# Attention values on Trainium2: float32 products on half of the array's columns for each head parity, in groups of four jobs

## The chip, the cores and the metric

The kernel runs on one core of one Trainium2 chip. A core has a matrix engine (TensorE: PE for its matmuls, PEld for its weight loads), three engines for elementwise work (VectorE: DVE; ScalarE: ACT; GpSimd: POOL) and an engine that issues transfers (SyncE: SP). Each engine works through its own queue in order and waits on semaphores for the others. The metric is the time of one execution on the device in microseconds (us); lower is better.

## The reference, cut to what matters

One decoder layer for 1024 tokens: a normalised input is projected, half of the heads go through sparse attention, the other half through a gated delta rule; an output projection and a gated MLP follow. The change concerns the attention. Each query sees three sets of keys: compressed blocks, selected blocks, and a window of 512 tokens. Each set has its own softmax, its own gate and its own values:

```
p_cmp = masked_softmax(einsum('bqhgd,bhnd->bhgqn', qb, kc), m_cmp)
o_cmp = einsum('bhgqn,bhnd->bqhgd', p_cmp, vc)
p_sel = masked_softmax(einsum('bqhgd,bhqnd->bhgqn', qb, k_sel), m_sel)
o_sel = einsum('bhgqn,bhqnd->bqhgd', p_sel, v_sel)
p_win = masked_softmax(einsum('bqhgd,bkhd->bhgqk', qb, kw), m_win)
o_win = einsum('bhgqk,bkhd->bqhgd', p_win, vw)
o = gate_cmp * o_cmp + gate_sel * o_sel + gate_win * o_win
```

There are 8 query heads of 64 numbers in 2 groups (g), each group with one key and one value head. All is float32.

## The kernel before, in words

The program goes through the stages input projections and delta rule, attention, output projection, MLP up, MLP down. In the attention a *unit* is 128 queries (tile i) of one group g with its four heads: 16 units, from tile 7 down to tile 0. `phase_attend` runs several units at once, one behind the other: `select` (compressed scores and the choice of blocks) of unit n+3, `scores` (the scores and softmax of the window and of the selection) of unit n+1, `values` of unit n, the norm of a finished tile, and `out_gdn` or `out_nsa` (part of the output projection, tile `og_ps`) as filler. `interleave` mixes them, and a scheduler then orders each engine's queue from what every instruction needs and from priorities; listings of that order stand with the change.

`values` gets the gated softmax rows as [128 queries, keys] and needs them with the keys on the partitions. Its work is a list of *jobs*: job 0 is the 64 compressed keys, then one job for each 128 keys of the window, then one for each 128 keys of the selection; 3 jobs for tile 0 up to 14 for tile 7, 148 in all units. A job before the change: four transposes on PE (L880, one a head) into one PSUM bank `pt` (three banks in rotation); ACT copies it rounded to the fast matmul format (L882, `ph`); DVE subtracts that copy from the bank to keep the rest (L890, `pl`; L885 for job 0); then PE does two products of 512 columns (L891 with `ph`, L892 with `pl`; L886 for job 0) into the one accumulator bank `po`. The values `vst` hold 128 columns: 64 rounded and 64 of the rest, so the two products give all four part products. At the end of a unit the halves of `po` are added and put into `oT` by head parity (heads 0 and 2 on partitions 0 to 63, heads 1 and 3 on 64 to 127): ACT copies one half or both (L897, L904), DVE or POOL adds (L899, L906).

The values are prepared before the attention: `v_raw` is loaded in four transfers, ACT rounds it (L613), POOL subtracts (L614). For the compressed values `compress` does the same from PSUM with ACT and DVE (L717, L718).

The delta rule uses plain float32 products too: `kk_ps` (L285) multiplies on one half of the array's columns for each half c of a token tile, and `u_ps` (L384) on all columns. A plain float32 product is two records of PE in the trace, each with a weight load of its own.

Of the kernel before, what the change touches and what calls it, by code (L numbers as in the profile page):

```python
# [9 lines left out]
F32 = mybir.dt.float32  # L10
F32R = mybir.dt.float32r
BF16 = mybir.dt.bfloat16
AF = mybir.ActivationFunctionType
ALU = mybir.AluOpType
# [4 lines left out]
P = 128  # L19
SEQ = 1024  # L20
NT = SEQ // P
# [487 lines left out]
def phase_in(K, ctx):  # L509
# [91 lines left out]
    K.vst = vp.tile([P, NT, 2, 2, P], F32R, name="vst")  # L601
# [6 lines left out]
    vr = scr.enter_context(tc.tile_pool(name="vraw", bufs=4, side="right"))  # L608
    for j in range(4):
        raw = vr.tile([P, 2, 2, 2, 64], F32, name="v_raw", tag="v_raw")  # L610
        nc.sync.dma_start(raw.rearrange("p t b g d -> p t (b g d)"), K.d_v[:, 2 * j:2 * j + 2, :])
        d = slice(2 * j, 2 * j + 2)
        nc.scalar.activation(K.vst[:, d, :, :, 0:64], raw, AF.Copy)  # L613
        nc.gpsimd.tensor_tensor(out=K.vst[:, d, :, :, 64:128], in0=raw, in1=K.vst[:, d, :, :, 0:64].bitcast(F32),  # L614
                                op=ALU.subtract)
# [46 lines left out]
def compress(K, which, pool):  # L662
# [47 lines left out]
    else:  # L710
        for h in range(2):
            vp = K.pp.tile([64, 64], F32, name="vc_ps", tag="proj")
            for j in range(2):
                nc.tensor.matmul(vp, x[:, j, 64 * h:64 * h + 64], w2[:, j, :], start=(j == 0), stop=(j == 1))

            for d in (slice(0, 64), slice(64, 128)):
                nc.scalar.activation(K.vc[d, h, 0:64], vp, AF.Copy, scale=0.5)  # L717
                nc.vector.scalar_tensor_tensor(out=K.vc[d, h, 64:128], in0=vp, scalar=0.5,  # L718
                                               in1=K.vc[0:64, h, 0:64].bitcast(F32), op0=ALU.mult, op1=ALU.subtract)
# [147 lines left out]
def values(K, i, g, U):  # L867

    nc = K.nc
    pc, pw, pn, lo = U.pc, U.pw, U.pn, U.lo  # L870
    po = K.p_o.tile([P, 4, P], F32, name="po", tag="po")
# [5 lines left out]
    for n, (src, v, kk) in enumerate(jobs):  # L877
        pt = K.p_t.tile([P, 4, P], F32, name="pt", tag="pt")
        for h in range(4):
            nc.tensor.transpose(pt[0:kk, h, :], src[h], K.ident)  # L880
        ph = K.apl.tile([P, 4, P], F32R, name="ph", tag="ph", bufs=3)
        nc.scalar.activation(ph[0:kk], pt[0:kk], AF.Copy)  # L882
        if n == 0:

            nc.vector.tensor_tensor(out=ph[kk:P], in0=pt[0:kk], in1=ph[0:kk].bitcast(F32), op=ALU.subtract)  # L885
            nc.tensor.matmul(po, v, ph, start=True, stop=False)  # L886
            yield
            continue
        pl = K.apl.tile([P, 4, P], F32R, name="pl", tag="pl", bufs=3)
        nc.vector.tensor_tensor(out=pl, in0=pt, in1=ph.bitcast(F32), op=ALU.subtract)  # L890
        nc.tensor.matmul(po, v, ph, start=False, stop=False)  # L891
        nc.tensor.matmul(po, v, pl, start=False, stop=(n == len(jobs) - 1))  # L892
        yield

    if i < 4:
        lo_ = K.apl.tile([64, 4, P], F32, name="po_s", tag="po_s", bufs=1)
        nc.scalar.activation(lo_, po[64:128], AF.Copy)  # L897
        for par in range(2):
            nc.vector.tensor_tensor(out=U.oT[64 * par:64 * par + 64, 2 * g:2 * g + 2, :], in0=po[0:64, par::2, :],  # L899
                                    in1=lo_[:, par::2, :], op=ALU.add)  # L900
        return
    hh = K.apl.tile([64, 2, 4, P], F32, name="po_s", tag="po_s", bufs=1)
    for j in range(2):
        nc.scalar.activation(hh[:, j], po[64 * j:64 * j + 64], AF.Copy)  # L904
    for par in range(2):
# [641 lines left out]
```

## Time and profile before

| | |
|---|---|
| time, median of 3 runs | 1500.3 us (1497.18 to 1500.89) |
| the profiled execution's own time | 1502.3 us |
| its span in the profile | 1500.5 us |
| PE busy | 1420.9 us (95%) |
| DVE busy | 1153.7 us (77%) |
| ACT busy | 723.3 us (48%) |
| POOL busy | 575.3 us (38%) |
| mean granted TensorE clock | 0.977 of full |

The span is the time from the first to the last instruction of the profiled execution; its own time is 1.8 us longer. Busy PE time includes the time in which a matmul drains while the next streams, so 95% doesn't mean that no time is left. The attention's values stand between 503 us (first transpose of `values`) and 792 us (last addition into `oT`) of the span.

### The profile page before, as it was taken

What the parts mean: (1) busy time and instruction counts of PE and PEld (TensorE: products, weight loads), DVE (VectorE), ACT (ScalarE), POOL (GpSimd) and SP (SyncE); (2) the same over time, 40 slices, a digit from 0 to 9 for tenths busy, and PEclk for the clock granted to TensorE, in tenths of its full rate; (3) what the DMA queues carried; (4) which work ended last, traced back from release to release, by engine and by line L of the source; (5) the groups of instructions that cost most, each with busy time, mean ns of one, the idle gap of its engine ahead of it and who ended that gap; (6) DMA issues with size and microseconds to landing.
All of it is one profiled execution on the core that took longest, in us unless ns stands there. A gap on an engine that the chain in (4) does not pass through costs nothing.

```text
span 1500.5 us, 21074 instructions
## 1 busy us (share of the span) xinstructions
PE 1420.9 (95%) x7260; PEld 1163.8 (78%) x7260; DVE 1153.7 (77%) x2222; ACT 723.3 (48%) x1405; POOL 575.3 (38%) x567
## 2 busy tenths in 40 slices
PE   8998899999989999989998979999999999989997
PEld 8876677787877777777787858888888888778886
DVE  5768997886335788898975797888888888687656
ACT  7443343232233566788865544444444445333333
POOL 3355433344352245466563541111111112364444
PEclk9999999999999999999999989999999999999999
DMA  6245352444366543132215112323222235773333
GB/s 234 87 156 177 107 169 72 125 121 150 93 219 173 161 138 112 58 85 52 55 64 200 40 70 105 105 105 106 105 94 98 97 105 194 268 267 87 103 106 147
DMA packets 106059, 188.04 MB, mean 125 GB/s; under 512 B 17216, under 2 KB 52064, under 8 KB 105952
## 3 DMA queue, kind: packets, MB, share of 16 engines
q1 hardware_dynamic: 105952, 186.69, 38.5%
q8 instruction: 57, 0.93, 0.3%
q14 instruction: 50, 0.41, 0.1%
HBM read 135.00 MB, written 51.66 MB: 124 GB/s over the span
## 4 chain that ended last, share of the span: by engine, by line
PE 64%; DVE 19%; DMA 6%; ACT 4%; issue 4%; POOL 2%; SPq 1%; DVEq 0%; ACTq 0%; POOLq 0%
PE up_ps L1130 27%; PE dn_ps L1328 11%; PE proj_ps L128 3%; PE proj_ps L126 3%; PE proj_ps L127 3%; DVE cv_acc L465 3%; PE pt L880 2%; DVE pl L890 2%; PE po L892 1%; DVE zb L350 1%; PE po L891 1%; DVE ztmp L348 1%; PE s_ps L820 1%; PE s_ps L415 1%; DMA d_x<-og 1%
## 5 line engine op out<-in xcount | busy, mean ns | idle before, releaser
L1328 PE MATMUL dn_ps<-d_op 128*128 128x512 f32 x924 | 211.4, 390 | 5.7 <-DVE d_op L1322 3.8
L1328 PEld LDWEIGHTS dn_ps<-d_op 128*128 128x128 f32 x924 | 173.0, 188 | 43.6 <-DVE d_op L1322 5.0
L128 PE MATMUL proj_ps<-hH,w_l 128*128 128x512 f32 x384 | 158.3, 412 | 6.6 <-POOL w_l L118 6.6
L126 PE MATMUL proj_ps<-hH,w_h 128*128 128x512 f32 x384 | 156.2, 408 | 5.0 <-ACT cv_acc L463 3.2
L127 PE MATMUL proj_ps<-hL,w_h 128*128 128x512 f32 x384 | 155.3, 405 | 0.1
L1320 POOL TENSOR_TENSOR d_op<-a_raw,d_op 128x1024 fp32r<-128x1024 f32 (+1 forms) x42 | 104.7, 2496 | 123.0 <-ACT d_op L1319 105.6
L1130 PE MATMUL up_ps<-th,op_h 128*128 128x512 f32 x336 | 133.5, 398 | 7.1 <-ACT op_h L1154 7.1
L1130 PE MATMUL up_ps<-th,op_l 128*128 128x512 f32 x336 | 133.6, 398 | 3.6 <-DVE op_l L1156 3.6
L1130 PE MATMUL up_ps<-tl,op_h 128*128 128x512 f32 x336 | 133.3, 397 | 0.0
L118 POOL TENSOR_TENSOR w_l<-w_raw,w_h 128x1024 fp32r<-128x1024 f32 (+2 forms) x46 | 110.1, 2398 | 46.1 <-ACT w_h L116 44.5
L1322 DVE TENSOR_TENSOR d_op<-b,d_op 128x1024 fp32r<-128x1024 f32 (+1 forms) x42 | 80.8, 1928 | 48.5 <-ACT d_op L1321 42.1
L1130 PE MATMUL up_ps<-dl,op_h 128*128 128x512 f32 x288 | 113.8, 395 | 0.0
L1130 PE MATMUL up_ps<-dh,op_h 128*128 128x512 f32 x288 | 112.6, 395 | 1.0 <-ACT acc L167 1.0
L1130 PE MATMUL up_ps<-dh,op_l 128*128 128x512 f32 x288 | 110.5, 394 | 0.0
L882 ACT ACTIVATE ph<-pt 128x512 fp32r<-128x512 f32 (+1 forms) x148 | 85.3, 591 | 49.1 <-PE pt L880 41.3
L1242 DVE SCALAR_TENSOR_TENSOR ga<-f_g,vec,ga 128x1024 f32<-128x1024 f32 x44 | 89.3, 2029 | 16.9 <-ACT ga L1240 16.3
L890 DVE TENSOR_TENSOR pl<-pt,ph 128x512 fp32r<-128x512 f32 x132 | 89.5, 683 | 9.1 <-ACT ph L882 8.6
L128 PEld LDWEIGHTS proj_ps<-hH,w_l 128*128 128x128 f32 x384 | 74.6, 194 | 26.9 <-POOL w_l L118 10.6
L1154 ACT ACTIVATE op_h<-w_raw 128x1024 fp32r<-128x1024 f32 (+1 forms) x64 | 59.0, 923 | 74.8 <-PE up_ps L1130 69.7
L1319 ACT ACTIVATE d_op<-a_raw 128x1024 fp32r<-128x1024 f32 (+1 forms) x42 | 41.4, 988 | 108.7 <-PE dn_ps L1328 53.8
L1175 POOL MEMSET f_u<- 128x2 f32 x22 | 2.2, 100 | 234.0 <-DVE acc L1242 233.1
L126 PEld LDWEIGHTS proj_ps<-hH,w_h 128*128 128x128 f32 x384 | 74.6, 195 | 21.2 <-ACT cv_acc L463 4.9
(343 smaller groups left out, 3654.6 us busy)
## 6 DMA issues: line engine op xcount, KB each, us to landing
w_raw<-in_w_up_dram SPq DMA_DIRECT2D x44, 512.0 KB, 3.2
a_raw<-d_a SPq DMA_DIRECT2D x35, 512.0 KB, 3.6
w_raw<-in_w_gdn_dram SPq DMA_DIRECT2D x24, 512.0 KB, 3.5
d_a<-ga SPq DMA_DIRECT2D x44, 256.0 KB, 2.0
b<-in_w_down_dram SPq DMA_DIRECT2D x20, 512.0 KB, 6.9
d_a<-so SPq DMA_DIRECT2D x33, 256.0 KB, 2.0
qT<-d_q SPq DMA_DIRECT2D x32, 256.0 KB, 4.8
mg<-d_mix SPq DMA_DIRECT2D x16, 512.0 KB, 3.7
```

Of the source, the lines that this page charges most:

```text
L118: (low or nc.gpsimd).tensor_tensor(out=wl, in0=raw, in1=wh.bitcast(F32), op=ALU.subtract)
L126: nc.tensor.matmul(out, ah, bh, start=(i == 0), stop=False)
L127: nc.tensor.matmul(out, ah, bl, start=False, stop=False)
L128: nc.tensor.matmul(out, al, bh, start=False, stop=(i == n - 1))
L882: nc.scalar.activation(ph[0:kk], pt[0:kk], AF.Copy)
L890: nc.vector.tensor_tensor(out=pl, in0=pt, in1=ph.bitcast(F32), op=ALU.subtract)
L1130: mm = lambda a, b, start, stop: nc.tensor.matmul(out, a, b, start=start, stop=stop, skip_group_check=not first)
L1154: nc.scalar.activation(h, src, AF.Copy)
L1242: nc.vector.scalar_tensor_tensor(out=a, in0=raw[:, j:j + SEQ], scalar=tap(j), in1=a, op0=ALU.mult, op1=ALU.add)
L1320: nc.gpsimd.tensor_tensor(out=al, in0=raw, in1=ah.bitcast(F32), op=ALU.subtract)
L1322: nc.vector.tensor_tensor(out=bl, in0=b[js.start], in1=bh.bitcast(F32), op=ALU.subtract)
L1328: one = lambda a, b, start, stop: nc.tensor.matmul(ps, a, b, start=start, stop=stop, skip_group_check=not first)
```

## The change

The value products become plain float32. `vst` holds the values once, 64 columns wide, and is filled by one transfer; `vc` holds the compressed values as 64 by 64 and is written by ACT alone. In `values` a transposed bank `pt` is copied once as float32 (`pT`), by DVE for the first job of each four and by ACT for the others. A product is split by head parity: heads 0 and 2 go with the value columns to partitions 0 to 63 of `po`, heads 1 and 3 to 64 to 127, each 256 columns wide. So `po` is already laid out as `oT`, and one copy by ACT ends the unit. The products of four jobs are issued one behind the other, newest job first, held in that order and with raised priority.

```
-    K.vst = vp.tile([P, NT, 2, 2, P], F32R, name="vst")
+    K.vst = vp.tile([P, NT, 2, 2, 64], F32, name="vst")
+    nc.sync.dma_start(K.vst.rearrange("p t b g d -> p t (b g d)"), K.d_v)
...
-    for j in range(4):
-        raw = vr.tile([P, 2, 2, 2, 64], F32, name="v_raw", tag="v_raw")
-        nc.sync.dma_start(raw.rearrange("p t b g d -> p t (b g d)"), K.d_v[:, 2 * j:2 * j + 2, :])
-        d = slice(2 * j, 2 * j + 2)
-        nc.scalar.activation(K.vst[:, d, :, :, 0:64], raw, AF.Copy)
-        nc.gpsimd.tensor_tensor(out=K.vst[:, d, :, :, 64:128], in0=raw, in1=K.vst[:, d, :, :, 0:64].bitcast(F32),
-                                op=ALU.subtract)
...
-            for d in (slice(0, 64), slice(64, 128)):
-                nc.scalar.activation(K.vc[d, h, 0:64], vp, AF.Copy, scale=0.5)
-                nc.vector.scalar_tensor_tensor(out=K.vc[d, h, 64:128], in0=vp, scalar=0.5,
-                                               in1=K.vc[0:64, h, 0:64].bitcast(F32), op0=ALU.mult, op1=ALU.subtract)
+            nc.scalar.activation(K.vc[:, h], vp, AF.Copy, scale=0.5)
...
-    po = K.p_o.tile([P, 4, P], F32, name="po", tag="po")
+    po = K.p_o.tile([P, 2, P], F32, name="po", tag="po")
...
-        ph = K.apl.tile([P, 4, P], F32R, name="ph", tag="ph", bufs=3)
-        nc.scalar.activation(ph[0:kk], pt[0:kk], AF.Copy)
...
-        pl = K.apl.tile([P, 4, P], F32R, name="pl", tag="pl", bufs=3)
-        nc.vector.tensor_tensor(out=pl, in0=pt, in1=ph.bitcast(F32), op=ALU.subtract)
-        nc.tensor.matmul(po, v, ph, start=False, stop=False)
-        nc.tensor.matmul(po, v, pl, start=False, stop=(n == len(jobs) - 1))
...
+    last, left = None, len(jobs)
+    for n0 in range(0, len(jobs), 4):
+
+        todo = []
+        for n in range(n0, min(n0 + 4, len(jobs))):
+            src, v, kk = jobs[n]
+            pt = K.p_t.tile([P, 4, P], F32, name="pt", tag="pt")
+            for h in range(4):
+                nc.tensor.transpose(pt[0:kk, h, :], src[h], K.ident)
+            pT = K.apl.tile([P, 4, P], F32, name="pT", tag="pT", bufs=2 * 4)
+            if n % 4 in (0,):
+                nc.vector.tensor_copy(pT[0:kk], pt[0:kk])
+            else:
+                nc.scalar.activation(pT[0:kk], pt[0:kk], AF.Copy)
+            todo.insert(0, (v, pT[0:kk]))
             yield
...
+        with tc.high_priority(offset=100):
+            for v, pT in todo:
+                left -= 1
+                for par in range(2):
+                    with tc.issue_after(last.ins) if last else nullcontext():
+                        last = nc.tensor.matmul(po[64 * par:64 * par + 64], v, pT[:, par::2], start=(last is None or first),
+                                                stop=(left == 0))
+                    first = par == 0 and left == len(jobs) - 1
+    nc.scalar.activation(U.oT[:, 2 * g:2 * g + 2, :], po, AF.Copy)
```

**PE in the first unit.** Before the change PE's queue stands so where the first jobs of tile 7's first unit are worked off (`pt` transposes, `po` value products, `s_ps` scores of the next unit, `og_ps` filler):

```order
L880 MATMUL pt<-ident,p_win 128x128 x4
L820 MATMUL s_ps<-kst_4414,qT 128x256
L822 MATMUL s_ps<-kst_4414,qT 128x256
L880 MATMUL pt<-ident,p_win 128x128 x4
L886 MATMUL po<-ph,vc 128x512
L891 MATMUL po<-ph,vst 128x512
L880 MATMUL pt<-ident,p_win 128x128 x4
L892 MATMUL po<-pl,vst 128x512
L891 MATMUL po<-ph,vst 128x512
L126 MATMUL og_ps<-w_h,mg 128x512
```

Now it stands so behind the transposes of the same unit's first four jobs (line numbers of the changed kernel: L877 transposes, L890 value products, one for each parity):

```order
L127 MATMUL og_ps<-w_l,mg 128x512
L128 MATMUL og_ps<-w_h,mg 128x512
L877 MATMUL pt<-ident,p_win 128x128 x4
L890 MATMUL po<-pT,vst 64x256 x6
L890 MATMUL po<-pT,vc 64x256 x2
L877 MATMUL pt<-ident,p_win 128x128 x4
L877 MATMUL pt<-ident,p_sel 128x128 x8
L809 MATMUL s_ps<-kst_4408,qT 128x384
L811 MATMUL s_ps<-kst_4408,qT 128x384
```

The two products of a job, which stood between transposes one job after its transposes, have become eight half-width products in one run, behind the transposes of the next group's first job. In the whole program PE has 41 such runs with 296 products; most hold four jobs.

**ACT at the end of a unit.** Before, where one unit ends and the next begins (`ph` copies of jobs, `po_s` the two halves of the accumulator, `p_win` softmax rows):

```order
L882 ACTIVATE ph<-pt 128x512
L904 ACTIVATE po_s<-po 64x512 x2
L838 ACTIVATE p_win,sums<-p_win,nmax 128x640
L882 ACTIVATE ph<-pt 128x512
L963 ACTIVATE mg<-mix 128x4x128
L882 ACTIVATE ph<-pt 128x512
L913 ACTIVATE sq<-oT 128x512
```

Now:

```order
L882 ACTIVATE pT<-pt 128x512
L741 ACTIVATE pc,sums<-pc,nmax 128x64 x2
L893 ACTIVATE oT<-po 128x256
L899 ACTIVATE sq<-oT 128x512
L882 ACTIVATE pT<-pt 128x512
L827 ACTIVATE p_win,sums<-p_win,nmax 128x640
```

The two copies of `po` are one of half the width that writes `oT` itself, and `sq`, the first step of the norm, stands right behind it; it no longer waits for an addition on another engine.

## Rows read from the trace of the kernel before

**Rows 1.** Windows: us, busy PE, PEld, DVE, ACT, POOL (x instructions), clock, DMA.

```profile
650.00:700.00 50.00, 46.30 (x292) 38.46 (x290) 46.10 (x154) 43.16 (x114) 32.19 (x44) 1.00 0.17 43
503.00:792.00 289.00, 267.78 (x1590) 222.55 (x1588) 247.94 (x810) 211.92 (x538) 149.44 (x217) 0.99 0.30 86
```

**Rows 2.** Groups by line, 503 to 792: busy us, mean ns, idle before.

```profile
L890 DVE TENSOR_TENSOR pl<-pt,ph 128x512 fp32r<-128x512 f32 x132 | 89.5, 683 | 9.1 <-ACT ph L882 8.6
L882 ACT ACTIVATE ph<-pt 128x512 fp32r<-128x512 f32 x132 | 76.8, 592 | 45.5 <-PE pt L880 38.0 <-PE po L886 6.1 <-DVE pl L890 0.5
...
L885 DVE TENSOR_TENSOR ph<-pt,ph 64x512 fp32r<-64x512 f32 x16 | 11.0, 685 | 1.4 <-ACT ph L882 1.0
...
L904 ACT ACTIVATE po_s<-po 64x512 f32<-64x512 f32 x16 | 9.5, 591 | 0.9 <-PE po L892 0.8
...
L899 DVE TENSOR_TENSOR oT<-po,po_s 64x256 f32<-64x256 f32 x16 | 6.6, 414 | 0.7 <-ACT po_s L897 0.6
...
L897 ACT ACTIVATE po_s<-po 64x512 f32<-64x512 f32 x8 | 4.8, 596 | 1.6 <-PE po L892 1.4
```

**Rows 3.** Waits of PE and PEld, 503 to 792: us in total, times, longest.

```profile
PE po L892 <- DVE pl L890: 6.8, 8, 1.9
PE pt L880 <- DVE og L952: 3.1, 4, 1.8
PE pt L880 <- DVE pl L890: 2.9, 3, 1.5
...
PEld po L892 <- DVE pl L890: 12.5, 18, 2.2
PEld pt L880 <- DVE pl L890: 2.6, 2, 1.7
```

**Rows 4.** Timeline around one stall: start us, us, engine, line.

```profile
663.30 0.60 PE L880 MATMUL pt<-ident,p_win 128*128 128x128 f32 x4
...
665.41 0.66 PE L880 MATMUL pt<-ident,p_win 128*128 128x128 f32 x4 [1.51 <-DVE pl L890]
...
664.68 0.68 DVE L890 TENSOR_TENSOR pl<-pt,ph 128x512 fp32r<-128x512 f32 x1
```

**Rows 5.** Timeline of PE, value products one behind the other.

```profile
666.38 0.39 PE L892 MATMUL po<-pl,vst 128*128 128x512 f32 x1
666.61 0.40 PE L891 MATMUL po<-ph,vst 128*128 128x512 f32 x1
```

**Rows 6.** Timeline of PE around one run of half-column float32 products.

```profile
109.21 0.39 PE L127 MATMUL proj_ps<-hL,w_h 128*128 128x512 f32 x1
109.53 1.09 PE L285 MATMUL kk_ps<-kq 128*64 128x128 f32 x16
110.55 0.50 PE L128 MATMUL proj_ps<-hH,w_l 128*128 128x512 f32 x1
110.89 0.40 PE L126 MATMUL proj_ps<-hH,w_h 128*128 128x512 f32 x1
```

**Rows 7.** Tile kk_ps, load and product: ns min/median/max.

```profile
L285 PEld LDWEIGHTS kk_ps<-kq x128: 132/137/137, 109.5 to 302.3; 128*64 128x64 f32 x128
L285 PE MATMUL kk_ps<-kq x128: 272/273/324, 109.5 to 302.4; 128*64 128x128 f32 x128
```

**Rows 8.** Full-width float32 products: timeline, and tile u_ps.

```profile
212.75 1.06 PE L384 MATMUL u_ps<-vv,Zx 128*128 128x128 f32 x8
...
L384 PE MATMUL u_ps<-vv,Zx x64: 274/275/377, 212.7 to 399.1; 128*128 128x128 f32 x64
```

**Rows 9.** Timeline at the end of the attention.

```profile
790.51 0.59 ACT L897 ACTIVATE po_s<-po 64x512 f32<-64x512 f32 x1 [1.38 <-PE po L892]
791.14 0.85 DVE L899 TENSOR_TENSOR oT<-po,po_s 64x256 f32<-64x256 f32 x2 [0.58 <-ACT po_s L897]
...
793.28 0.51 PE L126 MATMUL out_ps<-w_h,mh 128*128 128x512 f32 x1 [2.86 <-ACT mh L1037]
```

**Rows 10.** Waits of PE ahead of the attention, 400 to 512.

```profile
PE proj_ps L126 <- DVE vc L718: 1.6, 1, 1.6
```

More of the change, by code (lines that the diff above doesn't have):

```diff
@@ L1 @@
-from contextlib import ExitStack
+from contextlib import ExitStack, nullcontext
 import numpy as np
@@ L607, in phase_in @@
         nc.gpsimd.tensor_copy(K.masks[:, n], src)
-    vr = scr.enter_context(tc.tile_pool(name="vraw", bufs=4, side="right"))
-    for j in range(4):
-        raw = vr.tile([P, 2, 2, 2, 64], F32, name="v_raw", tag="v_raw")
-        nc.sync.dma_start(raw.rearrange("p t b g d -> p t (b g d)"), K.d_v[:, 2 * j:2 * j + 2, :])
-        d = slice(2 * j, 2 * j + 2)
-        nc.scalar.activation(K.vst[:, d, :, :, 0:64], raw, AF.Copy)
-        nc.gpsimd.tensor_tensor(out=K.vst[:, d, :, :, 64:128], in0=raw, in1=K.vst[:, d, :, :, 0:64].bitcast(F32),
-                                op=ALU.subtract)
     wk = scr.enter_context(tc.tile_pool(name="wk", bufs=2))
@@ L867, in values @@
 def values(K, i, g, U):
-    nc = K.nc
+    nc, tc = K.nc, K.tc
     pc, pw, pn, lo = U.pc, U.pw, U.pn, U.lo
-    po = K.p_o.tile([P, 4, P], F32, name="po", tag="po")
+    po = K.p_o.tile([P, 2, P], F32, name="po", tag="po")
     jobs = [([pc[:, h, :] for h in range(4)], K.vc[:, g, :], 64)]
@@ L876, in values @@
         jobs.append(([pn[h][:, k * P:(k + 1) * P] for h in range(4)], K.vst[:, k, 0, g, :], P))
[L877 to L880, printed above, removed]
-        ph = K.apl.tile([P, 4, P], F32R, name="ph", tag="ph", bufs=3)
-        nc.scalar.activation(ph[0:kk], pt[0:kk], AF.Copy)
-        if n == 0:
-            nc.vector.tensor_tensor(out=ph[kk:P], in0=pt[0:kk], in1=ph[0:kk].bitcast(F32), op=ALU.subtract)
-            nc.tensor.matmul(po, v, ph, start=True, stop=False)
-            yield
-            continue
-        pl = K.apl.tile([P, 4, P], F32R, name="pl", tag="pl", bufs=3)
-        nc.vector.tensor_tensor(out=pl, in0=pt, in1=ph.bitcast(F32), op=ALU.subtract)
-        nc.tensor.matmul(po, v, ph, start=False, stop=False)
-        nc.tensor.matmul(po, v, pl, start=False, stop=(n == len(jobs) - 1))
-        yield
@@ L895, in values @@
[L895 to L904, printed above, removed]
@@ L905, in values @@
-    for par in range(2):
-        nc.gpsimd.tensor_tensor(out=U.oT[64 * par:64 * par + 64, 2 * g:2 * g + 2, :], in0=hh[:, 0, par::2, :],
-                                in1=hh[:, 1, par::2, :], op=ALU.add)
+    last, left = None, len(jobs)
[12 more added lines that the diff above has]
+            todo.insert(0, (v, pT[0:kk]))
+            yield
+        with tc.high_priority(offset=100):
[6 more added lines that the diff above has]
+                    first = par == 0 and left == len(jobs) - 1
@@ L1442, in open_common @@
     K.kc = cp.tile([P, 2, 64], F32R, name="kc")
-    K.vc = cp.tile([P, 2, P], F32R, name="vc")
+    K.vc = cp.tile([64, 2, 64], F32, name="vc")
     K.ones = ep.tile([P, P], F32, name="ones")
```

## The prediction

> **What bounds the kernel now.** I read the stage table first, then the groups by line, then the waits of PE alone, and last the timeline at single stalls. The change touches the attention and what feeds it; from the MLP on the work is the same. So only the 289 us from 503 to 792 count, with a few us ahead of them and at their end. In these 289 us PE is busy for 267.8 us and DVE for 247.9, ACT for 211.9, POOL for 149.4; in the densest fifty PE and DVE stand at 46.3 and 46.1, ACT at 43.2 [rows 1]. No engine is far ahead of the others: PE does the most, and what keeps it from doing more is DVE. PE's idle time is 289 - 267.8 = 21.2 us, and its longest entry is the wait for `pl`, the subtraction on DVE: 6.8 us ahead of L892 and 2.9 us ahead of a transpose that needs its `pt` bank back, by the matmul records; 12.5 and 2.6 by those of the weight loads, which stand still from an earlier moment on [rows 3]. The stall at 665.41 shows the mechanism: the transposes at 663.30 were the last that found a free bank; the next ones had to stand for 1.51 us, until DVE, busy with softmax work until then, had done the subtraction that starts at 664.68 [rows 4]. So a bank is held for a copy on ACT and for a turn in DVE's queue.
>
> **What it takes from DVE, ACT and POOL.** DVE loses 132 subtractions of 0.683 us and 16 of 0.685, together 100.5 us, and 6.6 us of additions [rows 2]. It gains the copies of the first job of each four: 44 of them. DVE's plain copy of a 128x512 bank isn't in this stage; it reads one operand where the subtraction reads two, so 0.683 us bounds it from above (30 us), and half of that from below. Near the upper end DVE falls from 248 to about 171 us. ACT gives up 44 copies of 0.592 us (26 us) and 24 copies of `po` (14.3 us), and gains 16 of 128x256, at most 0.59 us each (9.5 us): 212 becomes about 181 us [rows 1, 2]. POOL loses 16 additions. None of these engines limits the stage by its sum afterwards, so this relief is worth only what PE waits for them.
>
> **What it does to PE.** Before: 280 value products that start 0.23 us apart where nothing holds them [rows 5], 64.4 us. After: 148 jobs with two parities, each a float32 product of 256 columns in two records. No such product is in the trace; the nearest is `kk_ps`, float32 on half of the columns, alternating halves, 128 columns wide. Its 16 records take 1.09 us; the last one lasts 0.273, so all start within 0.82 us [rows 6, 7]. On all columns `u_ps` has 8 records in 1.06 us, its last 0.275, so they start (1.06 - 0.275)/7 = 0.112 us apart [rows 8]. Sixteen in turn at that pace would need 15 x 0.112 = 1.68 us; at 0.82 the two halves go side by side, two records each 0.117 us with the start of the run in it. For 256 columns I double the 0.112: 0.224 us for a pair of records, two pairs a job, 148 x 0.448 = 66.3 us. That is 1.9 us more than before.
>
> What a run costs at its edges is in the same place: from the start of L127 at 109.21 to that of L126 at 110.89 are 1.68 us, of which two projection products take 0.46 and eight pairs 0.90; 0.32 us are lost between full and half columns, there and back [rows 6]. The order has 41 runs: 13.1 us. In 16 of them job 0 uses only 64 rows as well, which can cost another edge, 0 to 0.32 us each; its neighbours are in the same run, so I take none. PE's sum: +15 us (11 if neighbouring transposes hide part of the edges, 20 with all the extra edges).
>
> Here a rule of the Trainium skill speaks against the change. In rows, 16 loads of 0.137 us would be 2.2 us by themselves, and the run takes 1.09 in all, so loads lie beside products of the other half [rows 6, 7]. The Trainium skill, page "TensorE: Matmul & The Clock Gate", section "Part 3: Packing small matmuls — row/col tiling", says of what overlaps that weight loads run beside matmuls in flight only when their row groups differ; both halves here use all rows. By that rule the 592 loads would stand alone, some 81 us by the row's 0.137; by the rows they cost nothing. The trace disagrees with the page, and I go by the trace.
>
> **What PE gets back.** The waits for `pl` go, since nothing is subtracted any more and a bank is free after one copy: between 9.7 (6.8 + 2.9, matmuls) and 15.1 us (12.5 + 2.6, loads) [rows 3]. Smaller waits for `ph` go with them, so I take 15; bounds 10 and 20. What PE waits for other DVE work, such as `og` with 3.1 us [rows 3], shrinks with DVE's load, 248 to 171: idle time outside `pl` is 21.2 - 9.7 = 11.5 us, and I take half of it, 6 (0 to 11.5).
>
> **What is late next.** The first product of a run reads the newest copy of its group, on ACT, and behind it in PE's queue stand transposes, scores and filler of all the other units. In the order there is other PE work between the newest job's transposes and its run, mostly over 1.5 us; in the four tightest runs it is eight transposes, 8 x 0.11 = 0.9 us. A copy takes 0.592 us [rows 2], so with a free ACT no run waits; with a softmax row of the next unit ahead of it one could wait some 0.5 us. That bounds this cost at 0 and 41 x 0.5 = 20 us; ACT is busy for less than two thirds of the stage then, and I take 2, nearer to nothing.
>
> **Edges of the stage.** At its end the accumulator goes through ACT (0.59 us) and two additions on DVE (0.85 us) before PE goes on, idle for 2.86 us [rows 9]; one copy takes their place: -1 us (0 to -1.4). Ahead of it PE waits 1.6 us for `vc` on DVE, which goes [rows 10], and casts of `v_raw` no longer stand ahead of the last `q_h`: -2 (0 to -3), most of it that 1.6. The single load of `vst` is issued early and nothing is near it.
>
> The sum: +15 +2 -15 -6 -1 -2 = -7 us against the profiled execution's 1502.3: 1495.3. The median of the runs shown is 2.0 us below that execution, so 1493.3 there; I say 1493.
>
> **The rivals.** (A) As above, -4.5 to -15: 0.46. (B) DVE's relief frees more than the idle time that the waits name, since softmax rows come earlier for all units: all 21.2 us of idle go and the switches cost 11 with no new waits: 11 - 21.2 - 3 = -13 at the least, and down to -22 if starts that now lag without being shown as idle close up too: about 1480, 0.12. (C) PE is the bound itself: what it gets back, 15 + 6, is eaten by edges with the extra ones (20) and some waits: 0 us, 1500, 0.24. For it speaks that PE is already the busiest engine; against it that its idle time is nearly all DVE's. (D) Slower: ACT is behind, and the whole PE queue stands at the head of each run. It decides from 0.45 us a run on: 41 x 0.45 = 18.5 us in place of the 2, -7 + 16.5 = +9.5, 1510. For it speaks that the newest copy is read first, and that ACT had 43.2 us of 50 in the densest stretch; against it that PE has other work queued between: 0.13. (E) Halves or loads don't overlap at 256 columns: the loads alone +81 us, 1574; the halves in turn +66 us, 1559. Against it speaks the run of `kk_ps`: 0.05. The page's rule named above is this case.
>
> Within 0.3% (4.5 us) is about what a measurement of this kernel can tell from no change. Faster: A and B, 0.58; same: C, 0.24; slower: D and E, 0.18. The range leaves out E, the farther half of D and the far end of B: 1479 to 1509; A's own is 1485 to 1496.
>
> **What would show it.** Value products as pairs of records that start together, a pair each 0.22 us, and 41 gaps of about 0.3 us around them: PE's sum. No wait of PE for a DVE copy in the first places of the waits, DVE near 171 us and ACT near 181 in the stage: the relief. The stage then ends near 785 instead of 792 us, with its first transpose a little earlier. The prediction is wrong if the first product of runs waits for ACT by more than 0.4 us on average (D), if pairs are 0.4 us apart (E), or if PE's idle time hardly falls though `pl` is gone (C).

## The result, and the profile after

The changed kernel takes 1486.4 us (median of 4 runs, 1485.1 to 1486.5), the kernel before takes 1498.7 us (median of 4 runs next to them, 1497.1 to 1500.9). The ratio is 0.9915, with a 95% interval from 0.9898 to 0.9932: 12.4 us faster. Forecast were 1493 us, with faster as the likeliest case.

The head of the page after, busy time of each engine and its share of the span:

```profile
PE 1423.7 (96%) x7572; PEld 1144.8 (77%) x7572; DVE 1090.7 (74%) x2098; ACT 688.1 (46%) x1347; POOL 557.5 (38%) x547
```

The windows of the changed kernel that answer to [rows 1], the densest fifty and the whole of `values`:

```profile
496.00:773.00 277.00, 272.56 (x1905) 207.11 (x1903) 184.25 (x692) 180.46 (x487) 137.86 (x203) 0.99 0.31 90
650.00:700.00 50.00, 49.81 (x377) 37.36 (x375) 35.35 (x132) 40.31 (x114) 27.47 (x43) 1.00 0.20 43
```

The stage that took 289 us takes 277. DVE fell from 247.9 to 184.3 us and ACT from 211.9 to 180.5; PE, with 4.8 us more of busy time, is now idle for 4.4 us instead of 21.2. In the densest fifty PE has 49.8 of 50, DVE 35.4. So there is one bound now, where two stood side by side.

The waits of PE in the same stretch, answering to [rows 3]: the first three lines by the matmul records, then those of the load queue.

```profile
PE s_ps L809 <- DVE nmax L823: 2.1, 2, 1.7
PE pt L877 <- DVE og L938: 1.3, 4, 0.6
PE pt L877 <- ACT pT L882: 0.5, 1, 0.5
...
PEld po L890 <- issue: 11.1, 38, 0.4
PEld pt L877 <- issue: 8.8, 23, 0.4
...
PEld po L890 <- ACT pT L882: 0.6, 3, 0.3
```

The 6.8 and 12.5 us ahead of the second product are gone, and hardly anything took their place: runs wait 0.6 us for ACT's newest copy. The two `issue` lines are not waits for another engine. They come 38 times ahead of value products and 23 times ahead of transposes, 0.4 us at the longest. Before the change the same list had no such line ahead of a product, and this one ahead of transposes:

```profile
PEld pt L880 <- issue: 0.6, 3, 0.2
```

I read them as the edges between full and half columns; experiment 4 tests it.

The groups of the copies (answering to [rows 2]), and the product with its load by tile (answering to [rows 7]):

```profile
L882 ACT ACTIVATE pT<-pt 128x512 f32<-128x512 f32 x104 | 59.5, 589 | 48.3 <-PE pt L877 47.7
...
L880 DVE COPY pT<-pt 128x512 f32<-128x512 f32 x28 | 19.2, 686 | 2.3 <-ACT pT L882 1.9 <-PE pt L877 0.2
L880 DVE COPY pT<-pt 64x512 f32<-64x512 f32 x16 | 10.8, 674 | 0.0
...
L893 ACT ACTIVATE oT<-po 128x256 f32<-128x256 f32 x16 | 6.0, 378 | 9.6 <-PE po L890 9.5
```

```profile
L890 PEld LDWEIGHTS po<-pT,vst x528: 132/137/232, 502.5 to 771.1; 128*64 128x64 f32 x176
L890 PE MATMUL po<-pT,vst x528: 379/379/689, 502.5 to 771.3; 128*64 128x256 f32 x176
L890 PE MATMUL po<-pT,vc x64: 376/402/427, 503.9 to 771.9; 64*64 64x256 f32 x64
```

DVE's copy takes 0.686 us, as long as the subtraction that it replaced. One run of four jobs in the timeline of PE, with what stands on either side:

```profile
656.45 0.61 PE L877 MATMUL pt<-ident,p_sel 128*128 128x128 f32 x4
656.99 1.95 PE L890 MATMUL po<-pT,vst 128*64 128x256 f32 x16
658.87 0.50 PE L809 MATMUL s_ps<-kst,qT 128*128 128x512 f32 x1
```

Sixteen records in 1.88 us from first start to the next instruction. In the records behind this row they start in pairs, 7 ns apart within a pair and 0.216 us from pair to pair, so a job streams in 0.432 us; the 16 loads of 0.137 us (2.2 us) lie beside it. The end of the attention, answering to [rows 9]:

```profile
772.28 0.39 ACT L893 ACTIVATE oT<-po 128x256 f32<-128x256 f32 x1 [6.21 <-PE po L890]
...
773.78 0.47 PE L126 MATMUL out_ps<-w_h,mh 128*128 128x512 f32 x1 [0.88 <-ACT mh L1023]
```

Where the time went, from first and last starts in the two profiled executions (spans 1500.5 and 1483.3 us):

| | before | after | change |
|---|---|---|---|
| up to the first transpose of `values` | 502.8 | 496.4 | -6.4 |
| first transpose to last product (the stage, from here on) | 287.1 | 275.5 | -11.6 |
| last product to first `out_ps` | 3.4 | 1.9 | -1.5 |
| first `out_ps` to first `up_ps` | 28.7 | 26.4 | -2.4 |
| first `up_ps` to first `dn_ps` | 446.9 | 450.5 | +3.6 |
| first `dn_ps` to last `dn_ps` | 222.0 | 223.3 | +1.3 |

The changes are worked out before rounding and sum to -17.0 us. The medians differ by 12.4 only, since the profile of before lies 3.6 us above its median and that of after 1.3 below. The first row is the one that varies: the same changed kernel, profiled again (below), had its first transpose at 501.1 us. The stage varies less: it took 274.0 to 276.9 us in the four profiles that have these value products unchanged (the changed kernel twice, and the two versions of experiment 6).

DVE was to fall to about 171 us and fell to 184.3, while ACT came out at the 181 us forecast. The durations of DVE's single instructions do sum to 76 us less in the stage (299.0 and 223.2), as counted in the prediction; but the records overlap in time, so its busy time fell by 63.7 only.

### The profile page after: what moved, and what is told of

The parts are those of the page before. It is cut to its first block, busy times and chain, and to the rows that moved or that the text cites. A ratio compares the mean times of both kernels' runs of the same rounds, so it can differ in the third digit from the quotient of the medians.

```text
span 1483.3 us, 21381 instructions
## 1 busy us (share of the span) xinstructions
PE 1423.7 (96%) x7572; PEld 1144.8 (77%) x7572; DVE 1090.7 (74%) x2098; ACT 688.1 (46%) x1347; POOL 557.5 (38%) x547
## 4 chain that ended last, share of the span: by engine, by line
PE 67%; DVE 16%; DMA 6%; issue 4%; ACT 4%; POOL 2%; SPq 0%; DVEq 0%; ACTq 0%; POOLq 0%
PE up_ps L1116 27%; PE dn_ps L1314 10%; PE po L890 4%; PE pt L877 4%; DVE cv_acc L465 3%; PE proj_ps L128 2%; PE proj_ps L126 2%; PE proj_ps L127 2%; PE s_ps L809 2%; PE s_ps L811 2%; DVE zb L350 1%; DVE ztmp L348 1%; PE og_ps L126 1%; PE og_ps L127 1%; PE og_ps L128 1%
## 5 line engine op out<-in xcount | busy, mean ns | idle before, releaser
L1228 DVE SCALAR_TENSOR_TENSOR ga<-f_g,vec,ga 128x1024 f32<-128x1024 f32 x44 | 91.0, 2068 | 11.1 <-ACT ga L1226 10.4
L128 PEld LDWEIGHTS proj_ps<-hH,w_l 128*128 128x128 f32 x384 | 74.1, 193 | 27.0 <-POOL w_l L118 10.9
L465 DVE SCALAR_TENSOR_TENSOR cv_acc<-cv_raw,vec,cv_acc 128x512 f32<-128x512 f32 x72 | 76.6, 1063 | 18.4 <-ACT cv_acc L463 17.6
L127 PEld LDWEIGHTS proj_ps<-hL,w_h 128*128 128x128 f32 x384 | 74.2, 193 | 15.6 <-DVE hL L188 0.4
```

The lines of the kernel that those rows point to most:

```text
L127: nc.tensor.matmul(out, ah, bl, start=False, stop=False)
L128: nc.tensor.matmul(out, al, bh, start=False, stop=(i == n - 1))
L465: nc.vector.scalar_tensor_tensor(out=acc, in0=raw[:, j:j + 512], scalar=tap(j), in1=acc, op0=ALU.mult, op1=ALU.add)
L1228: nc.vector.scalar_tensor_tensor(out=a, in0=raw[:, j:j + SEQ], scalar=tap(j), in1=a, op0=ALU.mult, op1=ALU.add)
```

## The experiments

All are edits of the changed kernel; times are medians beside runs of the kernel before on the same chip. A stage is measured as in the table.

**1. DVE's load given back.** Theory: DVE's load as such cost PE time. Rival: only the banks did, held for a turn on DVE.

```
                 nc.scalar.activation(pT[0:kk], pt[0:kk], AF.Copy)
+                pj = K.apl.tile([P, 4, P], F32, name="pj", tag="pj", bufs=2)
+                nc.vector.tensor_tensor(out=pj[0:kk], in0=pT[0:kk], in1=pT[0:kk], op=ALU.subtract)
```

> After each copy on ACT, DVE subtracts the copy from itself into a buffer that nobody reads: 104 operations of 128x512 on data of the copy alone, so that no accumulator bank is held for them; only DVE's load returns (about 184 + 104 x 0.68 = 255 us in the stage, as before the change). Theory: what the change gained in the attention came from DVE's load as much as from the bank; the time goes back by more than half of the stage's gain of 13 us: 1494 to 1505 us. Rival: the gain came from the bank pt, which no longer waits for its turn on DVE; DVE's load as such costs little: 1486 to 1490 us.

Measured: 1502.3 us, ratio 1.0008 (0.9993 to 1.0023), so the whole gain is gone. Its window over the stage:

```profile
495.00:784.00 289.00, 276.28 (x1902) 207.64 (x1900) 246.44 (x796) 179.32 (x485) 157.66 (x203) 0.99 0.30 86
```

DVE stands at 246.4 us, as before the change, and the stage takes 288.5 us, 13.0 more than in the changed kernel. No one waits for `pj`. DVE's 62 us more came back as 13 us of PE's time, spread over waits for `og`, for softmax steps and smaller ones:

```profile
PE pt L877 <- DVE og L940: 4.8, 4, 1.7
PE s_ps L809 <- DVE nmax L739: 2.4, 1, 2.4
```

POOL's busy time rose as well, from 137.9 to 157.7 us, but in the next run it stands at 138.0 and the stage is as long, so POOL isn't the cause. The theory holds, near its upper end.

**2. The bank held as well.** The same, but the subtraction reads `pt`, so a bank comes free only after DVE.

```
-                nc.vector.tensor_tensor(out=pj[0:kk], in0=pT[0:kk], in1=pT[0:kk], op=ALU.subtract)
+                nc.vector.tensor_tensor(out=pj[0:kk], in0=pt[0:kk], in1=pT[0:kk], op=ALU.subtract)
```

> As the run before with DVE's load given back, but the 104 subtractions on DVE read the transposed bank pt itself and ACT's copy, as the subtraction of the kernel before did; so a bank is free only after its turn on DVE. Nobody reads the result. Now the attention has the old load of DVE and the old hold on the banks, and the new products on PE alone are left of the change. Theory: this shows what the new products cost PE: from the first start of a run to the next instruction's start the runs take 73.8 us in all, the old products 64.4; with the load of DVE alone the stage had 288.9 us, with the bank too it gets about 298, and the time is about 1511 us. Rival 1: the bank costs nothing beside DVE's load: 1502 us as with the load alone. Rival 2: the edges cost the full 13 us and more: stage 305 us, 1518 us.

Measured: 1501.0 us, ratio 1.0005 (0.9983 to 1.0027); stage 287.3 us. The theory missed and rival 1 holds: no loss from the bank beyond DVE's load that can be told, which the two intervals bound at some 4 us. Yet the waits by the matmul records do name the bank. The window over the stage, and these waits:

```profile
498.00:787.00 289.00, 276.18 (x1907) 207.37 (x1905) 241.35 (x796) 179.45 (x487) 138.03 (x204) 1.00 0.30 86
```

```profile
PE pt L877 <- DVE pj L884: 4.4, 5, 1.2
PE s_ps L809 <- DVE nmax L823: 2.5, 3, 2.0
PE pt L877 <- DVE og L940: 2.5, 4, 1.3
```

A transpose now waits 4.4 us for `pj`; without that hold PE waited as long in other places. A wait in such a list is the one that ended last, and its length is not the time that its removal gives back.

**3. Products behind DVE again.** Both runs left a question. With DVE's load and the hold on the bank returned, the stage is as long as before the change, so the new products seem to be free. Here the products also read DVE's output, as the low product read `pl`. DVE takes the greater of the bank and its copy, which are equal, so the numbers stay.

```
                 nc.vector.tensor_copy(pT[0:kk], pt[0:kk])
+                pj = pT
...
+                pj = K.apl.tile([P, 4, P], F32, name="pj", tag="pj", bufs=6)
+                nc.vector.tensor_tensor(out=pj[0:kk], in0=pt[0:kk], in1=pT[0:kk], op=ALU.max)
-            todo.insert(0, (v, pT[0:kk]))
+            todo.insert(0, (v, pj[0:kk]))
```

> As the two runs with DVE's load given back, but the products of those 104 jobs read what DVE writes: DVE takes the greater of pt and ACT's copy of it (the two are equal, so the numbers stay) into a buffer pj, and the product reads pj. So each job again goes transposes, ACT, DVE, product, as the subtraction pl did before the change. In the two earlier runs DVE's load alone took back 12 to 13 us of the attention, and the hold on the bank nothing more; yet the stage was then no longer than before the change (287 us), though by the slope over 25, 41 and 79 runs of products (0.23 us a run) the new products cost PE some 11 us. Theory: the missing 11 us are the products' own wait for the subtraction (12.5 us by the records of the loads, before the change); in this run it is back, and the stage takes 295 to 300 us, the time is 1508 to 1514 us, and PE waits at po for pj. Rival: in groups of four that wait is hidden by the work between; 287 to 289 us, 1501 us.

Measured: 1508.0 us, ratio 1.0049 (1.0027 to 1.0070); stage 298.2 us, 10.9 more than in the run before this and 11.1 more than in the kernel before. Its window, and its waits by the load queue:

```profile
495.00:794.00 299.00, 284.01 (x1907) 211.35 (x1905) 239.81 (x800) 181.13 (x487) 138.71 (x204) 0.97 0.29 83
```

```profile
PEld pt L877 <- DVE pj L885: 5.2, 7, 2.0
...
PEld po L893 <- DVE pj L885: 4.5, 14, 0.5
```

The size is as the theory said, but the form is not. Products wait 4.5 us for `pj` by the load records, yet against experiment 2 PE's idle time grows by only 2.2 us (15.0 and 12.8) and its busy time by 7.8: a granted clock of 0.97 over the stage, where experiment 2 had 1.00, lengthens the products. In times the step is 1.0049 against 1.0005, 6.6 us with intervals that touch at 1.0027. So the run in which products wait for a second engine is 7 to 11 us longer; how much of that is the wait and how much the clock is not separated, and whether the waits bring the lower clock about is not shown.

**4. What an edge costs.** Groups of two, eight and single jobs; the split of the copies between DVE and ACT stays. The version with eight has ten buffers for the copies instead of eight.

```
-    for n0 in range(0, len(jobs), 4):
+    for n0 in range(0, len(jobs), 2):
...
-        for n in range(n0, min(n0 + 4, len(jobs))):
+        for n in range(n0, min(n0 + 2, len(jobs))):
```

> Groups of two jobs instead of four (the split of the copies between DVE and ACT stays): PE has 79 runs of products instead of 41. Theory: a run costs 0.32 us at its edges, as predicted from kk_ps; 38 more runs are +12 us, 1498 us. Rival 1: an edge costs about half of that, since loads of the next transposes hide a part: +6, 1492 us. Rival 2: the runs of four matter because a run waits for its newest copy; with two the waits come twice as often, and waits of PE for ACT appear in the first places: more than +15 us, over 1501 us.

> Groups of eight jobs instead of four (ten buffers for the copies): PE has 25 runs instead of 41. Theory: 38 more runs cost 4 to 7 us in the run with groups of two, 0.1 to 0.2 us each; 16 fewer runs give back 2 to 3 us: 1483 to 1485 us. Rival: longer runs let the banks fill and the copies wait for their buffers, or they keep the softmax of the next units from starting, so that the gain is lost: 1488 to 1495 us.

> Each job's products are issued for themselves (the split of the copies stays): PE has 119 runs of products instead of 41. Theory: 0.20 to 0.23 us a run, from the stage lengths with 41 and 79 runs (275.5 and 283.2 us) and with 25 (271.0): 78 more runs are +16 to +18 us, stage 291 to 294 us, time 1501 to 1504 us. Rival 1: only what lies inside the runs is paid (73.8 and 78.2 us for 41 and 79 runs, 0.12 us a run); the rest of the 7.7 us was something else: stage about 285 us, 1495 us. Rival 2: a single job's product waits for its own copy; PE waits for ACT or DVE at po in many runs, and the stage is over 296 us.

| jobs a group | runs on PE | stage, us | ratio (95%) |
|---|---|---|---|
| 8 | 25 | 271.0 | 0.9887 (0.9843 to 0.9932) |
| 4 (the changed kernel) | 41 | 275.5 | 0.9915 (0.9898 to 0.9932) |
| 2 | 79 | 283.2 | 0.9940 (0.9918 to 0.9962) |
| 1 | 119 | 292.1 | 1.0043 (1.0028 to 1.0057) |

The three times are 1483.4, 1491.2 and 1504.1 us. The window of the version with single jobs, its waits by the load queue, and a piece of PE's timeline:

```profile
496.00:790.00 294.00, 291.79 (x1907) 200.17 (x1905) 186.81 (x693) 180.05 (x487) 139.03 (x204) 1.00 0.29 85
```

```profile
PEld pt L877 <- issue: 33.1, 86, 0.4
PEld po L890 <- issue: 16.8, 66, 0.4
...
PEld po L890 <- ACT pT L882: 1.2, 5, 0.4
```

```profile
647.14 0.65 PE L890 MATMUL po<-pT,vst 128*64 128x256 f32 x4
647.73 0.66 PE L877 MATMUL pt<-ident,p_sel 128*128 128x128 f32 x4
```

Hardly anything waits for a copy (1.2 us); what grew is `issue`. The stage grows by 16.6 us for 78 runs, 0.213 us a run. It grows by 0.20 a run for the 38 between four and two, and by 0.28 for the 16 between eight and four. So the theory of 0.32 us a run misses for groups of two, its rival of about half holds better, and the rivals with waits fall, as does the one by which single jobs pay 0.12 us a run. Carried on to no run at all, which nobody measured, 41 runs cost 41 x 0.213 = 8.7 us. In the timeline one job, 0.432 us of streaming, takes 0.59 us from its first start to the next transpose's. As whole times groups of eight are not told apart from groups of four.

**5. The halves one after the other.** All products of the first parity, then all of the second.

```
-            for v, pT in todo:
...
-                for par in range(2):
+            for par in range(2):
+                for m, (v, pT) in enumerate(todo):
```

> In each run all products of the first head parity are issued, then all of the second, so that neighbouring products write to the same half of the columns. Theory: the float32 products are cheap because two halves stream side by side; a pair of records starts every 0.216 us in the changed kernel, and in series each record needs that time for itself. 592 records x 0.216 = 127.9 us in place of 63.9: about +60 us, 1546 us. Rival 1: the records only follow one another and the halves don't matter; 1486 us. Rival 2: the weight loads (0.137 us each) come out into the open as well: +60 + 81, about 1627 us.

Measured: 1531.4 us, ratio 1.0204 (1.0169 to 1.0239), where the theory had 1546. A run of four jobs without job 0 and one with it, each with the transposes behind it:

```profile
645.36 2.86 PE L891 MATMUL po<-pT,vst 128*64 128x256 f32 x16
648.15 1.09 PE L877 MATMUL pt<-ident,p_win 128*128 128x128 f32 x8
...
651.45 1.51 PE L891 MATMUL po<-pT,vst 128*64 128x256 f32 x6
...
653.46 1.51 PE L891 MATMUL po<-pT,vst 128*64 128x256 f32 x6
...
655.48 0.66 PE L877 MATMUL pt<-ident,p_sel 128*128 128x128 f32 x4
```

The mean run of four jobs takes 3.42 us here and 1.99 in the changed kernel; all runs together 122.0 and 73.8 us (first start to the next instruction's), and the stage 321.9. The halves do stream side by side when they alternate, and that is worth 48 us in the runs, where the theory had 127.9 - 63.9 = 64. The mean of 3.42 us mixes two kinds. Without job 0 a run takes 2.79 us (15 runs): on one half records start 0.216 us apart, but the first record of the second half starts beside the fifth of the first, so four records of each half still go side by side, 15 x 4 x 0.216 = 13 us in all. With job 0 a run takes 4.02 us (median of 13): the two records on 64 rows stand at the end of each half, nothing overlaps, and from start to start around them it is 0.27 to 0.31 us. The loads stay hidden here too, so rival 2 falls: 592 x 0.137 = 81 us didn't come.

**6. The work ahead of the attention.** First all of the old preparation, then only that of the compressed values.

```
-    nc.sync.dma_start(K.vst.rearrange("p t b g d -> p t (b g d)"), K.d_v)
+    for j in range(4):
+        raw = vr.tile([P, 2, 2, 2, 64], F32, name="v_raw", tag="v_raw")
...
+            for d in (slice(0, 64), slice(64, 128)):
+                nc.scalar.activation(K.vc[d, h, 0:64], vp, AF.Copy, scale=0.5)
+                nc.vector.scalar_tensor_tensor(out=K.vc[d, h, 64:128], in0=vp, scalar=0.5, in1=K.vc[0:64, h, 0:64],
+                                               op0=ALU.mult, op1=ALU.subtract)
```

> The new value products stay; the work ahead of the attention is that of before again: four loads of v_raw, their copies on ACT and subtractions on POOL, and the two copies on ACT and two subtractions on DVE for each compressed value tile (the second halves are written and not used). In the changed kernel the first transpose of the values comes 6.4 us earlier than before (496.4 instead of 502.8 us), where 2 us were predicted. Theory: all of this comes from the removed preparation; the first transpose goes back to 502 to 503 us and the time to 1492 to 1493 us. Rival: only the wait for vc (1.6 us) belongs to the preparation and the rest to the order in which the first units start; the first transpose stays near 498 us and the time is 1487 to 1489 us.

> Only the compressed values are prepared as before (two copies on ACT and two subtractions on DVE each, the second halves not used); vst stays one load. In the trace of before the wait for vc is 1.6 us, and behind it ten projection products start 0.43 us apart at a granted clock of 0.50, in the changed kernel only five do. Theory: the wait brings this back: first product behind it 1.5 us later and five more at half clock, 1 us; the wait for qT and the half-clock stretch behind it at 459 to 462 us, which came with the loads of v_raw, stays away. Last proj_ps 2 to 3 us later than the 467.2 us of the changed kernel. Rival: the half clock doesn't hang on this wait: only 1.5 us later, or less.

Measured: all of it 1490.4 us, ratio 0.9931 (0.9907 to 0.9955), first transpose at 500.9 us and last `proj_ps` at 471.0. Only the compressed values: 1494.0 us in a single run, first transpose at 503.7, last `proj_ps` at 471.9 (467.2 in the changed kernel). As whole times neither is told apart from the changed kernel. The last `proj_ps` came 4.7 us later with `vc` alone, where 2 to 3 were expected. What the traces show is the wait for `vc`, and the granted clock behind it. Windows of the kernel before, of the changed one, and of the one with only `vc` as before (columns as in [rows 1]):

```profile
419.00:425.00 6.00, 4.42 (x13) 3.36 (x12) 2.35 (x8) 3.00 (x14) 5.11 (x4) 0.50 0.57 175
455.00:470.00 15.00, 13.42 (x58) 10.77 (x57) 4.69 (x15) 3.81 (x12) 0.96 (x1) 0.89 0.86 197
```

```profile
419.00:425.00 6.00, 5.91 (x23) 4.66 (x22) 1.70 (x4) 2.76 (x12) 5.67 (x5) 0.78 0.59 209
455.00:470.00 15.00, 13.90 (x70) 11.68 (x70) 7.90 (x35) 4.73 (x15) 0.72 (x2) 1.00 0.76 184
```

```profile
419.00:425.00 6.00, 4.60 (x15) 3.54 (x14) 2.26 (x8) 2.93 (x14) 5.20 (x4) 0.52 0.50 165
455.00:470.00 15.00, 13.04 (x56) 10.63 (x55) 4.24 (x15) 3.73 (x12) 0.00 (x0) 0.89 0.73 169
```

And the first product behind the wait, in the kernel before and in the changed one:

```profile
420.88 0.79 PE L126 MATMUL proj_ps<-hH,w_h 128*128 128x512 f32 x1 [1.58 <-DVE vc L718]
...
422.32 0.63 PE L126 MATMUL proj_ps<-hH,w_h 128*128 128x512 f32 x1
422.75 0.63 PE L127 MATMUL proj_ps<-hL,w_h 128*128 128x512 f32 x1
```

```profile
419.36 0.79 PE L126 MATMUL proj_ps<-hH,w_h 128*128 128x512 f32 x1
...
422.15 0.39 PE L127 MATMUL proj_ps<-hL,w_h 128*128 128x512 f32 x1
422.37 0.40 PE L128 MATMUL proj_ps<-hH,w_l 128*128 128x512 f32 x1
```

The clock is at 0.50 (the lower of its two levels, 1.2 GHz) when `vc_ps` ends, in both kernels. In the changed one it rises within five products; with the wait it stays there to nearly 425 us, and a projection product starts every 0.43 us instead of every 0.23. A second such stretch follows the wait for `qT` at 459 us. In all three profiles with the old `vc` there are nine intervals of about 0.43 us behind `vc_ps` and seven or eight behind `qT`. In the eleven with the new one, the changed kernel twice among them, eight have 4 to 9 behind `vc_ps` and none behind `qT`, three none and seven. The totals don't overlap, but nine stand behind `vc_ps` in one profile without the wait too (copies on ACT, experiment 7), so the wait doesn't set the length of that stretch alone. First transposes lie at 500.9 to 503.7 us (mean 502.5) against 494.8 to 501.1 (mean 497.7): 4.8 us between the means, with ranges that touch, and with the loads of `v_raw` no visible part of it. So the old `vc` goes with the late start; with three profiles, and one run of the version with `vc` alone, the cause is likely and not shown. That the second stretch would stay away with `vc` alone put back, as expected, was wrong. The wait of PE for `qT` was 1.58 to 2.35 us in the six profiles with the second stretch and 0.39 to 1.57 in the eight without it. Why the one is followed by half clock and the other not stays open, and so does what makes that wait longer.

**7. Copies on ACT, and the version with eight jobs.** All copies of `pt` on ACT; then this with groups of eight and twelve buffers; and the changed kernel once more on the chip of that version.

```
-            if n % 4 in (0,):
+            if n % 4 in ():
```

> All 148 copies of pt go to ACT, none to DVE: DVE loses 44 x 0.68 = 30 us (184 to about 154 in the stage), ACT gains 44 x 0.59 = 26 us (180 to 206). Theory: with the change PE is busy for 98% of the stage and is the bound; less load on DVE gives nothing more, and ACT still has a quarter of the stage free: 1485 to 1490 us. Rival 1: DVE's load still costs in proportion (14 us for the 62 us that were given back before): -6, about 1480 us. Rival 2: ACT becomes late, and runs wait for their newest copy: over 1493 us.

> Groups of eight jobs (twelve buffers) and all copies of pt on ACT. Theory: an edge costs about 0.23 us, so 25 runs instead of 41 give back 3 to 4 us in the attention, as in the run with groups of eight (stage 271 us instead of 275.5); the load that moves from DVE to ACT changes nothing more: 1481 to 1484 us. Rival: with the copies on one engine a run of eight waits for its newest copy, or its banks come free later; 1486 us and more.

> The changed kernel itself, on the same chip as the two others, to compare the version with eight jobs directly and to see the start of the attention once more. 1486 us, if the chips agree. The last proj_ps near 465 to 468 us and the first transpose of the values near 495 to 498 us, with five half-clock products behind vc_ps and none behind the wait for qT; where it shows more of them, as one run without the wait for vc did (seven, behind qT), it comes 2 to 4 us later.

Measured: copies on ACT 1484.8 us, ratio 0.9909 (0.9874 to 0.9945), stage 274.8; eight jobs and ACT 1486.5 us, 0.9897 (0.9872 to 0.9922), stage 277.1; the changed kernel again 1487.4 us, 0.9917 (0.9896 to 0.9938), stage 276.4. The window with all copies on ACT:

```profile
498.00:774.00 276.00, 271.98 (x1903) 207.03 (x1901) 160.13 (x647) 199.61 (x532) 137.16 (x201) 0.99 0.32 90
```

Taking another 24 us of busy time from DVE gives nothing that can be measured, where giving it 62 us cost 13: at 184 us and less DVE no longer bounds the stage. Where between 184 and 246 us it begins to, no run shows. The changed kernel again had its first transpose at 501.1 us, where 495 to 498 was expected, with no half clock behind `vc_ps` and seven such intervals behind `qT`. With eight jobs and one engine for the copies the stage of the one profile is 6 us longer than with eight jobs alone. Its waits by the load queue name softmax steps and copies:

```profile
PEld s_ps L809 <- DVE nmax L823: 4.4, 4, 1.7
PEld po L890 <- ACT pT L882: 2.6, 6, 0.9
```

So the theory missed the stage by 6 us; 6.8 us of it also ran at a granted clock of 0.50, and what ate the saved edges is not separated. No version here beats the changed kernel by more than the measurement can tell.

## Why the prediction was right, and which sizes were off

The mechanism was right: PE's own cost rises and its waits on DVE fall by more. In the windows PE's busy time rose by 4.8 us and its idle time fell by 16.8. That the time fell into A's range was partly luck: the 6 us for DVE's other work were half of an idle time, taken without a measurement, and of the rows below six came out lower than summed, by 13 us together, and two higher, by 5. By terms:

| term of the sum | predicted | measured | by |
|---|---|---|---|
| streaming of the products | +1.9 | -0.5 | 148 x 0.432 against 64.4 |
| edges of 41 runs | +13.1 | +8.7 | 0.213 us a run, experiment 4 |
| waits for the newest copy | +2 | +0.6 | load queue after |
| 64-row products of job 0 | 0 (to 5) | +2.4 | 1.88 and 2.03 us a run |
| waits for `pl`, and for DVE's other work | -15, -6 | -22.8 | what is left of the stage's -11.6 |
| the stage's end | -1 | -1.5 | table of stages |
| ahead of the stage | -2 | -4.8 (-6.4 in the profiles) | experiment 6 |
| behind the attention | none | +2.5 in the profiles | table of stages |

The rows sum to -15.4 us, 3 more than the medians differ by. They come from single profiles, so none is good to better than about 1 us. The edges rest on the slope of experiment 4, and the -22.8 is a remainder that takes up whatever the other rows have wrong.

**PE's cost.** The overlap of halves and the hidden loads, read from `kk_ps`, hold at 256 columns, and 0.216 us a pair was read to within 4%. The step that was mis-sized is the edge: 0.32 us had been read from one run in which nothing stood between projection products of 512 columns; in the attention an edge costs 0.213 us. Job 0's 64 rows, taken as free, cost 0.15 us a run: runs of four jobs take 1.88 us without job 0 and 2.03 with it. In all PE's cost was +10.6 us where +15 had been summed (11 at the least).

**What PE got back.** -21 was predicted and -22.8 came, but the split was off. The text gave 15 us to the waits for `pl` and 6 to DVE's lighter load. Experiment 1 puts 13 us on DVE's load; the rest, 10 us, fits the products' own wait for a second engine (experiment 3: 7 to 11, clock included), but no run shows it by itself. A part of it is the clock: in the stage before, 6.8 us ran at a granted clock of 0.50 (from 568.4 and from 623.0 us), after the change 3.4 us (from 636.7), which is at most 1.7 us of work. The part of the mechanism that fell is the bank: the stall at 665 us [rows 4] was read as a bank held for a turn on DVE, and holding it again cost nothing that can be told beside the load (experiment 2). The reading that fits is that DVE was late with everything, and whichever instruction stood next in PE's queue showed the wait. DVE's fall to 171 us was a difference of summed durations set against a busy time in which records overlap; it came to 184.3.

**Ahead of the stage.** Of the 2 us, 1.6 were the wait for `vc` [rows 10]. Left out was the clock behind it: in the two profiles compared, four more intervals of 0.43 us instead of 0.23 are 0.8 us, and seven or eight behind `qT` another 1.5. Behind the attention 2.5 us are lost again in the profiles. PE's waits in the first part of the MLP sum to 13.2 us after and 11.7 before, and the rest lies in no single wait; but the stretch that takes 446.9 us before and 450.5 after takes 446.4 to 452.0 in the profiles of the experiments, so one profile of each can't tell the two kernels apart there. Ahead of the MLP, the output projection runs at 0.94 granted clock before and 1.00 after; before, it begins behind a wait of 2.9 us [rows 9], now behind one of 0.88.

**The rivals.** The time is in A's range, just short of B's near end (-13), and by terms it lies between them: PE's cost of 10.6 us is B's 11 and not A's 15, and of the idle time that B lets go whole 4.4 us are left. C would have needed the edges at their upper end and an idle time that hardly falls. D fell: 0.6 us of waits where 18.5 were its condition. E fell in experiment 5. There the rule of the Trainium skill that stood against the change, page "TensorE: Matmul & The Clock Gate", section "Part 3: Packing small matmuls — row/col tiling", was on trial: that loads run beside products in flight only when their row groups differ. All loads here use the same rows as the products beside them, save those of job 0. Those others are 528 at 0.137 us, 72 us in all; but for the first of a run they stayed hidden whether the halves alternated or not, since records kept 0.216 us from start to start in both. For this kernel the measurement decides against the rule as that sentence of the section puts it.

## What to carry to other kernels

Where two engines stand side by side at the top, don't add up the waits that the profile names; give an engine its load back in a buffer that nobody reads, and measure. Here 62 us of load on DVE were worth 13 us of PE's time, while the bank that a stall named was worth nothing that could be told. And take an engine's new load from its busy time with care: where its records overlap, the sum of the durations that go is more than the busy time that goes. Splitting a product by column halves pays when neighbours alternate between the halves (73.8 against 122.0 us here), and grouping pays about 0.2 us for each run of half-column products that it avoids (a change there and one back), as long as nobody waits for the last operand of the group. A short wait of PE ahead of a dense stretch can go with a cost above its length: look at the start-to-start times of the products behind it.

## What the hardware showed unexpectedly

- Short waits of PE and half clock came together. Behind the wait of 1.58 us for `vc` nine intervals of about 0.43 us stood between products that otherwise start 0.23 us apart, where the profiles without that wait had 0 to 9. Waits for `qT` of 1.58 to 2.35 us were followed by seven or eight such intervals in six profiles, waits of 0.39 to 1.57 us by none in eight.
- With one half of the columns after the other, the first record of the second half started beside the fifth of the first (0.92 us into a run of 2.79 us); where two records on 64 rows stood between, it waited for the last of them.
- An edge between full-width and half-column products costs 0.213 us there and back in the attention, by 119 and 41 runs, where one run of `kk_ps` had shown 0.32 [rows 6].
- DVE's plain copy of a 128x512 bank takes 0.686 us, no less than the subtraction with two operands (0.683) [rows 2].
